# Retention and cross attention in a decoder step: the low weight parts on VectorE, the sample's rows turned later, the last products by token halves

## The chip, the cores and the metric

One core of one Trainium2 chip runs the whole step in one program. Its engines are TensorE (PE, with its weight loads as PEld), VectorE (DVE), ScalarE (ACT), GpSimd (POOL) and SyncE (SP, which only issues transfers here). Each engine works its own instructions in order and waits for others by semaphores. The metric is the device time of one execution in microseconds, lower is better.

## The reference

One step of a decoder of two layers, on 512 prompt tokens and 8 x 8 sample tokens, 576 token columns in all, with 1024 channels. Layer 0 mixes tokens by retention, layer 1 by causal pooling; each then attends to 256 memory tokens (cross attention, four heads of 256) and runs a gated feed-forward part with a short convolution. Cut to what bears on the change:

```python
def retention_mixer(h, pos, s0, w_in, gn_g, w_out):
    proj = h @ w_in                       # q, k, v, g of 4 heads
    q, k = rope(...), rope(...) * RET_DK ** -0.5
    o, s = retention_chunks(q, k, v, s0, chunk)      # chunks of 128 tokens
    o = ((o - mu) * lax.rsqrt(var + GN_EPS)).reshape(B, L, hv) * gn_g
    return (jax.nn.silu(g) * o) @ w_out, s

def cross_attn(h, k, v, wq, wo):
    q = (h @ wq).reshape(B, L, X_HEADS, X_HEAD_DIM)
    p = jax.nn.softmax(jnp.einsum('blhd,bmhd->bhlm', q, k) * X_HEAD_DIM ** -0.5, axis=-1)
    return jnp.einsum('bhlm,bmhd->blhd', p, v).reshape(B, L, D_MODEL) @ wo
```

All inputs and outputs are float32.

## The kernel before

Channels lie on the 128 partitions and tokens along the free axis, the 64 sample tokens first. A float32 product is made of three passes of a faster TensorE format: every operand is split into a high part (a cast, on ScalarE) and a low part (source minus high part), and `mm3` adds high x high, high x low and low x high. `split` writes both parts. `load_w` does it for each weight tile of 128x1024: a transfer to `wraw`, the cast to `wh` (L229), and the subtraction to `wl` (L230). The subtraction is on VectorE, except where `W.lo` is 1: there it is on GpSimd. `W.lo` is 1 while the tasks of a cross stage are run (L1184 to L1187), of which there are two, one per layer.

The 576 columns of a product are two pieces of PSUM, one of 320 (sample and the first 256 prompt tokens) and one of 256, called the token halves. `mm_kt` makes one step: one output tile of 128 channels, one 128-deep slice of the input, both halves, three passes: two `wh` matmuls and one `wl` matmul per half.

The order in which PE works is set by code. A main list of tasks (projections and the products that follow) hands over after every step, and side generators (`B` side of a head: the sample's recurrent state; out side: the prompt's chunks; in the cross stages one side per pair of heads) are called between them. A side says with `yield t` after how much estimated PE work, in microseconds, it wants to be called again; `Weave` keeps the clock of these estimates. A scheduler then places each engine's instructions; tiles of a pool with `bufs=n` can hold a program's instruction back until one of n slots is free.

In the retention the sides of head h end in the same way. `normed` (from L635) takes the statistics of a 128x512 result in PSUM on VectorE and writes the normed tile `on` on ScalarE (L642), with two slots. `gate_out` turns `on` by four transposes on PE (L219), multiplies it by the gate on VectorE into `yt`, and stores it (heads 0 to 2) or splits it into `qhl` and `khl` (head 3). The sample does this in `b_side`, each of four prompt chunks in `out_side`.

`out_tasks` is the product with `w_out`: four groups of two output tiles, and four parts of the input per group, one per head. The first group's fourth part uses head 3's fresh `qhl` and `khl`; its eight steps go output tile by output tile, each with both halves.

A cross stage computes the query tiles (`ev_q`: `qt` on VectorE, its split into `qo`, a copy of the sample's columns into `Z` on GpSimd), runs the attention of prompt and sample as sides (`ph`, `pl` are the parts of the turned probabilities or keys, `pT` the turned probabilities, `mx`, `sm` belong to the softmax), and multiplies by `w_xo`, which adds to the residual `x` (L1162, or L417 for whole tiles) and feeds the norm of the next stage (`sqacc` and `xhl`).

Of the kernel before, what the change touches and what calls it, by code (L numbers as in the profile page):

```python
# [156 lines left out]
def body(ctx, tc, a, cdec):  # L157
# [4 lines left out]
    def f(t):  # L162
        return t.bitcast(F32)
# [17 lines left out]
    def acc():  # L181
        return P.acc.tile([128, 1024], F32, tag="acc", name=nm("acc"))

    def tp():
        return P.tp.tile([128, 512], F32, tag="tp", name=nm("tp"))

    def new(p, shape, tag, dt=F32, whole=True, **kw):


        n = 1  # L190
        for s in shape[1:]:
            n *= s
        o = LINE // 2 if tag in ODD else 0
        if n % LINE == 0 and o == 0 or not whole:
            return p.tile(shape, dt, tag=tag, name=nm(tag), **kw)
        t = p.tile([shape[0], -(-(n + o) // LINE) * LINE], dt, tag=tag, name=nm(tag), **kw)[:, o:o + n]
        if len(shape) == 2:
            return t
        ax = "abcd"[:len(shape) - 1]
        return t.rearrange(f"p ({' '.join(ax)}) -> p {' '.join(ax)}", **dict(zip(ax[1:], shape[2:])))  # L200

    def token_rows(p, shape, tag):

        return new(p, shape + [ROW], tag, F32R)[:, :, :, ROW - NT:]
# [7 lines left out]
    def mm(out, lhsT, rhs, start, stop):  # L212
        i = nc.tensor.matmul(out, lhsT, rhs, start=start, stop=stop)  # L213
        if not wv.inside:
            wv.last = i.ins
        wv.now += max(cols(rhs) / 2340.0, 0.107)
# [5 lines left out]
    def mm3(out, lh, ll, rh, rl, start, stop):  # L222
        mm(out, lh, rh, start, False)
        mm(out, lh, rl, False, False)
        mm(out, ll, rh, False, stop)

    def split(hi, lo, src, scale=None, lo_pool=False):
        if scale is None:
            act.copy(hi, src)  # L229
            (pool if lo_pool else dve).tensor_tensor(out=lo, in0=src, in1=f(hi), op=ALU.subtract)  # L230
        else:
            act.activation(hi, src, AF.Copy, scale=scale)
            dve.scalar_tensor_tensor(out=lo, in0=src, scalar=scale, in1=f(hi), op0=ALU.mult, op1=ALU.subtract)  # L233
# [16 lines left out]

    class W:
        pool = first = None
        lo = 0

    def load_w(src, shape):

        raw = new(W.pool, shape, "wraw", bufs=W.raw_bufs)
        dma.dma_start(out=raw, in_=src)
        wh = new(W.pool, shape, "wh", F32R, bufs=W.hl_bufs)
        wl = new(W.pool, shape, "wl", F32R, bufs=W.hl_bufs)  # L260
        split(wh, wl, raw, lo_pool=W.lo)
        return wh, wl

    def w_cols(w, r0, nk, c0):
# [17 lines left out]
    def two_cols(w, *cs):  # L282
        return lambda: [w_cols(w, 0, KT, c) for c in cs]
# [130 lines left out]
    def add_x(norm=None):  # L414
        def evac(i, ps):
            x = xt["x"]
            dve.tensor_tensor(out=x[:, i], in0=x[:, i], in1=flat(ps), op=ALU.add)  # L417
            if norm is not None:
                norm.feed(i)
        return evac  # L420
# [216 lines left out]
    def normed(o):  # L637

        mv, rs, nb = gn_stats(o, 128)
        on = new(ap, [128, 512], "on", bufs=2)  # L640
        dve.tensor_scalar(out=nb, in0=mv[:, 0:1], scalar1=rs, scalar2=-1.0, op0=ALU.mult, op1=ALU.mult)
        act.activation(on, o, AF.Identity, scale=rs, bias=nb)  # L642
        return on
# [80 lines left out]
    def b_side(h):  # L724

        s = hd[h]
        vst = s["vst"]
        S = {}
        order = [(4 * g + j, k2) for g in range(2) for k2 in range(2) for j in range(4)]

        def state(t, u):
            b, k2 = order[u]
            return t[0, b, h, 128 * k2:128 * k2 + 128]

        def load(u):
            if u < 2 * B:
                S[u] = new(ap, [128, DV], "S", bufs=10)
                dma.dma_start(out=S[u], in_=state(a["state_ret"], u))

        for u in range(8):  # L740
            load(u)
        yield 4.5
        pso = tp()
        mm(pso, As, s["vs32"], True, False)
        yield 0.3
        for u in range(2 * B):
            b, k2 = order[u]
            if u % 4 == 0:
                for j in range(4):
                    c = 128 * (b // 4) + 32 * j  # L750
                    mm(pso[32 * j:32 * j + 32], Z[:, k2, c:c + 32], S[u + j], False, u == 2 * B - 4)
            psu = tp()
            mm(psu, kst[:, b, 128 * k2:128 * k2 + 128], vst[:, b // 4], True, True)
            Su = S.pop(u)
            dve.scalar_tensor_tensor(out=Su, in0=Su, scalar=cdec[h], in1=psu, op0=ALU.mult, op1=ALU.add)  # L755
            dma.dma_start(out=state(a["o_ret_s"], u), in_=Su)
            load(u + 8)
            yield 1.7
        on = normed(pso)
        yield 6.0  # L760
        gate_out(h, on, 0)

    def out_side(h):

        s = hd[h]
        A, vhl = s["A"], s["vhl"]
        ons = {}
        for qc in range(5):
            if qc < 4:
                ps = tp()  # L770
                for kc in range(qc + 1):
                    o = AOFF[kc] + 128 * (qc - kc)
                    mm3(ps, A[:, 0, o:o + 128], A[:, 1, o:o + 128], vhl[:, 0, kc], vhl[:, 1, kc], kc == 0, kc == qc)
                ons[qc] = normed(ps)
                yield 6.0
            if qc > 0:
                gate_out(h, ons.pop(qc - 1), NS + 128 * (qc - 1))
                yield 0.5
# [111 lines left out]
    def out_tasks():  # L890
        tasks = []
        evac = add_x(first_norm)
        for grp in range(4):
            hold = {}
            for part, k0 in enumerate((8, 0, 4, 12)):
                def run(wt, part=part, k0=k0, grp=grp, hold=hold):
                    if part == 0:
                        if grp == 0:
                            wv.join(hd[3]["y2"])
                        hold.update({0: acc(), 1: acc()})  # L900
                    if grp == 0 and part == 1:
                        ya = token_rows(gp, [128, 2, KT], "xhl")
                        for ft in range(8):
                            y_load(ft, ya[:, 0, ft], ya[:, 1, ft])
                    if grp == 0 and part == 3:
                        wv.join(hd[3]["out"], hd[3]["bl"])
                        for i in range(4):
                            yk[12 + i] = y3[i // 2][:, 0, i % 2], y3[i // 2][:, 1, i % 2]
                        sA.close()
                        xt["pool"] = xp = open_pool(sX, "xp")  # L910
                        xt["x"] = new(xp, [128, KT, NT], "x")
                        for kt in range(KT):
                            dma.dma_start(out=xt["x"][:, kt], in_=x_dram[:, kt])
                        W.pool = open_pool(sX, "wB")
                        W.raw_bufs, W.hl_bufs = 3, 3
                    wh, wl = wt
                    if grp == 3 and part == 3:
                        first_norm.gcol = G_XA
                        for kt in range(4):
                            first_norm.split(kt)  # L920
                    for m, kt in [(m, kt) for kt in range(4) for m in range(2)] if part < 3 else \
                            [(m, kt) for m in range(2) for kt in range(4)]:
                        cc = slice(128 * m, 128 * m + 128)
                        mm_kt(hold[m], (wh[:, :, cc], wl[:, :, cc]), kt, *yk[k0 + kt], part + kt == 0,
                              part == 3 and kt == 3)
                        yield
                        if part == 3 and kt == 3:
                            evac(2 * grp + m, hold[m])
                            if grp == 3 and m == 0:
                                first_norm.split(4)  # L930
                                first_norm.split(5)

                tasks.append(Task(lambda k0=k0, grp=grp: w_rows(w_out, 128 * k0, 4, 256 * grp, 256), run))
        return tasks

# [12 lines left out]
    def cross(l, norm, nnext):  # L948
        with ExitStack() as sp, ExitStack() as s:
# [231 lines left out]
            t0 = wo_tasks(0, (lambda: (wv.join(sides[0][0]), sides[1].append(wv.spawn(prompts_side(1)))),  # L1181
                              lambda: wv.join(*sides[0])))
            t1 = wo_tasks(1, (lambda: wv.join(sides[1][1]), lambda: wv.join(*sides[1])), nnext)
            W.lo = 1  # L1184
            wv.run(run_tasks(tasks + t0 + t1, two_cols(a["w_up"][l], 0, DFF)))
            wv.drain()
            W.lo = 0  # L1187


    def ffn(l, norm, nnext=None, side=None, then=None):  # L1190
# [370 lines left out]
```

## Time and profile before

| | us |
|---|---|
| median of 3 runs | 1900.1 |
| lowest, highest | 1899.54, 1905.7 |
| the profiled execution | 1899.72 |
| its span | 1897.9 |
| PE busy | 1859.6 |
| DVE busy | 1055.9 |
| ACT busy | 734.7 |
| POOL busy | 272.4 |

The span runs from the first to the last instruction of the profile. By place: retention heads from about 80 to 525 us, the product with `w_out` to 615, the first cross stage to 786, feed-forward 0 to 1150, memory and pooling to 1285, the second cross stage to 1464, feed-forward 1 to the end. An engine that is busy for nearly all of the span sets the time; for the others only the moments count at which that engine waits for them.

### The profile page before, as it was taken

Reading aid. Unit: us, or ns where it says so; the run is one execution under the profiler, and the core shown is the slowest. Engines: PE = TensorE matmul, PEld = TensorE weight load, DVE = VectorE, ACT = ScalarE, POOL = GpSimd, SP = SyncE. Lnnn points to the kernel's source line nnn. Section 1 sums busy time; section 2 is a strip of 40 time slices with the busy share of each in tenths; the row PEclk is TensorE's granted clock in tenths of the full one; section 3 lists DMA queues with packets and bytes.
Section 4 is the critical chain, followed back from the end, with each engine's and each line's share of the span. In section 5 each row is a group of like instructions: output and inputs, shape, how many; then the busy total and the mean of one; then the engine's idle time right before and its main releaser. Section 6 shows DMA issues by size and latency. Waiting matters only on the chain.

```text
span 1897.9 us, 32670 instructions
## 1 busy us (share of the span) xinstructions
PE 1859.6 (98%) x13493; PEld 1742.7 (92%) x13493; DVE 1055.9 (56%) x1607; ACT 734.7 (39%) x1080; POOL 272.4 (14%) x416
## 2 busy tenths in 40 slices
PE   7999999999999999999999999999999999999998
PEld 6888888888899888899999999988898999999998
DVE  5635445464634554676366367674555673564567
ACT  5442332424423433443234134554443442342345
POOL 0211102021000312211011010003212210110010
PEclk9999999999999999999999999999999999999999
DMA  8645363555733555232322322546543223232224
GB/s 288 206 135 177 97 217 114 173 163 159 242 111 105 170 176 167 79 101 79 89 87 82 90 78 76 182 139 212 188 157 115 84 79 89 80 87 86 82 73 142
DMA packets 309691, 249.52 MB, mean 131 GB/s; under 512 B 12136, under 2 KB 267992, under 8 KB 309543
## 3 DMA queue, kind: packets, MB, share of 16 engines
q1 hardware_dynamic: 309543, 247.44, 42.3%
q8 instruction: 106, 1.74, 0.4%
q14 instruction: 42, 0.34, 0.1%
HBM read 210.51 MB, written 36.88 MB: 130 GB/s over the span
## 4 chain that ended last, share of the span: by engine, by line
PE 88%; DMA 3%; DVE 3%; issue 2%; ACT 2%; POOL 1%; SPq 0%; ACTq 0%; POOLq 0%; DVEq 0%
PE acc L213 74%; PE tp L213 11%; PE tp L219 3%; DMA kvr<-in_cache_mem_v 1%; DMA wraw<-in_w_xk 1%; DVE qo L230 1%; ACT wh L229 1%; DVE wl L230 1%; DMA wraw<-in_w_xq 0%; DMA cs<-in_c_rope 0%; ACT qo L229 0%; DVE xhl L233 0%; DMA y<-in_p_conv 0%; POOL r L602 0%; POOL wl L230 0%
## 5 line engine op out<-in xcount | busy, mean ns | idle before, releaser
L213 PE MATMUL acc<-xhl,wh 128*128 128x320 f32 (+1 forms) x4608 | 919.6, 295 | 2.2 <-ACT m4k L473 1.0
L213 PEld LDWEIGHTS acc<-xhl,wh 128*128 128x128 f32 x4608 | 737.8, 188 | 13.4 <-issue 6.7
L213 PE MATMUL acc<-xhl,wl 128*128 128x320 f32 (+1 forms) x2304 | 674.8, 293 | 0.0
L229 ACT CAST wh<-wraw 128x1024 fp32r<-128x1024 f32 (+1 forms) x274 | 281.3, 1030 | 644.6 <-PE acc L213 508.9
L213 PEld LDWEIGHTS acc<-xhl,wl 128*128 128x128 f32 x2304 | 434.0, 188 | 0.0
L230 DVE TENSOR_TENSOR wl<-wraw,wh 128x1024 fp32r<-128x1024 f32 (+1 forms) x242 | 293.3, 1215 | 131.9 <-ACT wh L229 126.1
L213 PE MATMUL acc<-yhl,wh 128*128 128x320 f32 (+1 forms) x1408 | 278.7, 295 | 0.1
L213 PEld LDWEIGHTS acc<-yhl,wh 128*128 128x128 f32 x1408 | 223.7, 188 | 0.5 <-ACT yhl L229 0.4
L213 PE MATMUL acc<-yhl,wl 128*128 128x320 f32 (+1 forms) x704 | 205.8, 293 | 0.0
L1234 DVE SCALAR_TENSOR_TENSOR c<-e,cw,c 128x592 f32<-128x592 f32 x176 | 145.9, 832 | 3.8 <-ACT c L1232 0.3
L213 PEld LDWEIGHTS acc<-yhl,wl 128*128 128x128 f32 x704 | 132.6, 188 | 0.0
L417 DVE TENSOR_TENSOR x<-x,acc 128x576 f32<-128x576 f32 x64 | 48.2, 753 | 148.2 <-PE acc L213 148.0
L230 POOL TENSOR_TENSOR wl<-wraw,wh 128x1024 fp32r<-128x1024 f32 x32 | 78.5, 2452 | 287.0 <-ACT wh L229 247.7
L213 PE MATMUL acc<-qo,wh 128*128 128x320 f32 (+1 forms) x512 | 108.0, 305 | 6.1 <-DVE x L1162 5.5
L213 PE MATMUL acc<-wh,xhl 128*128 128x512 f32 (+1 forms) x320 | 96.4, 374 | 0.0
L213 PEld LDWEIGHTS acc<-qo,wh 128*128 128x128 f32 x512 | 82.2, 191 | 12.7 <-DVE x L1162 6.4
L213 PE MATMUL acc<-wh,mT 128*128 128x512 f32 x256 | 86.1, 405 | 3.1 <-ACT wh L229 3.1
L1232 ACT ACTIVATE c<-e,cw 128x592 f32<-128x592 f32 x88 | 77.6, 884 | 21.0 <-DVE e L1227 20.6
L1225 DVE TENSOR_TENSOR e<-acc,rstd_bc 128x64 f32<-128x64 f32 x88 | 19.5, 222 | 114.4 <-PE acc L213 114.2
L1228 POOL COPY cb<-e 128x16 f32<-128x16 f32 x88 | 18.8, 214 | 422.4 <-DVE e L1225 422.4
L213 PE MATMUL acc<-qo,wl 128*128 128x256 f32 (+1 forms) x256 | 75.8, 299 | 0.0
L755 DVE SCALAR_TENSOR_TENSOR S<-S,tp 128x512 f32<-128x512 f32 x64 | 43.6, 682 | 52.6 <-PE tp L213 46.7
(281 smaller groups left out, 2328.9 us busy)
## 6 DMA issues: line engine op xcount, KB each, us to landing
wraw<-in_w_up SPq DMA_DIRECT2D x88, 512.0 KB, 3.7
wraw<-in_w_ret_in SPq DMA_DIRECT2D x48, 512.0 KB, 4.4
S<-in_state_ret SPq DMA_DIRECT2D x64, 256.0 KB, 4.1
o_ret_s<-S SPq DMA_DIRECT2D x64, 256.0 KB, 3.5
kvr<-in_cache_mem_k SPq DMA_DIRECT2D x64, 256.0 KB, 4.1
kvr<-in_cache_mem_v SPq DMA_DIRECT2D x64, 256.0 KB, 3.5
wraw<-in_w_down SPq DMA_DIRECT2D x32, 512.0 KB, 3.8
wraw<-in_w_down SPq DMA_DIRECT2D x24, 384.0 KB, 3.3
```

Source lines behind the costliest of these rows:

```text
L213: i = nc.tensor.matmul(out, lhsT, rhs, start=start, stop=stop)
L219: nc.tensor.transpose(out, in_, idn)
L229: act.copy(hi, src)
L230: (pool if lo_pool else dve).tensor_tensor(out=lo, in0=src, in1=f(hi), op=ALU.subtract)
L417: dve.tensor_tensor(out=x[:, i], in0=x[:, i], in1=flat(ps), op=ALU.add)
L755: dve.scalar_tensor_tensor(out=Su, in0=Su, scalar=cdec[h], in1=psu, op0=ALU.mult, op1=ALU.add)
L1225: dve.tensor_tensor(out=ev[:, 0:8, 2:10], in0=ps[:, A0:A0 + NS].rearrange("p (b t) -> p b t", t=T), in1=rstd_bc[:, 0:NS].rearrange("p (b t ...
L1228: pool.tensor_copy(cb[:, 0:16, j].rearrange("p (b t) -> p b t", t=2), ev[:, 0:8, 8:10])
L1232: act.activation(c, e[:, 2:2 + n], AF.Identity, scale=cw[:, 2, j:j + 1], bias=cw[:, 3, j:j + 1])
L1234: dve.scalar_tensor_tensor(out=c, in0=e[:, i:i + n], scalar=cw[:, i, j:j + 1], in1=c, op0=ALU.mult, op1=ALU.add)
```

## The change

Three edits. First, `W.lo` goes: the low parts of the weights loaded in the cross stages are written by VectorE like all others, 32 tiles of 128x1024. Second, the numbers in the sides' `yield` change: the sample's rows are turned after 8.5 instead of 6.0 us of estimated PE work (5.0 in head 3), and the prompt's chunks of head 3 after 4.5 instead of 6.0. Third, the fourth part of the first group of `out_tasks` runs all its steps for the first token half and then all for the second.

```diff
--- before.py
+++ after.py
@@ -250,7 +250,6 @@
 
     class W:
         pool = first = None
-        lo = 0
 
     def load_w(src, shape):
 
@@ -258,7 +257,7 @@
         dma.dma_start(out=raw, in_=src)
         wh = new(W.pool, shape, "wh", F32R, bufs=W.hl_bufs)
         wl = new(W.pool, shape, "wl", F32R, bufs=W.hl_bufs)
-        split(wh, wl, raw, lo_pool=W.lo)
+        split(wh, wl, raw)
         return wh, wl
 
     def w_cols(w, r0, nk, c0):
@@ -757,7 +756,7 @@
             load(u + 8)
             yield 1.7
         on = normed(pso)
-        yield 6.0
+        yield 8.5 if h < 3 else 5.0
         gate_out(h, on, 0)
 
     def out_side(h):
@@ -772,7 +771,7 @@
                     o = AOFF[kc] + 128 * (qc - kc)
                     mm3(ps, A[:, 0, o:o + 128], A[:, 1, o:o + 128], vhl[:, 0, kc], vhl[:, 1, kc], kc == 0, kc == qc)
                 ons[qc] = normed(ps)
-                yield 6.0
+                yield 6.0 if h < 3 else 4.5
             if qc > 0:
                 gate_out(h, ons.pop(qc - 1), NS + 128 * (qc - 1))
                 yield 0.5
@@ -918,13 +917,19 @@
                         first_norm.gcol = G_XA
                         for kt in range(4):
                             first_norm.split(kt)
-                    for m, kt in [(m, kt) for kt in range(4) for m in range(2)] if part < 3 else \
-                            [(m, kt) for m in range(2) for kt in range(4)]:
+                    both = (0, 1)
+                    steps = [(m, kt, both) for kt in range(4) for m in range(2)]
+                    if part == 3:
+                        steps = [(m, kt, both) for m in range(2) for kt in range(4)]
+                        if grp == 0:
+
+                            steps = [(m, kt, (hv,)) for hv in both for m in range(2) for kt in range(4)]
+                    for m, kt, halves in steps:
                         cc = slice(128 * m, 128 * m + 128)
                         mm_kt(hold[m], (wh[:, :, cc], wl[:, :, cc]), kt, *yk[k0 + kt], part + kt == 0,
-                              part == 3 and kt == 3)
+                              part == 3 and kt == 3, halves)
                         yield
-                        if part == 3 and kt == 3:
+                        if part == 3 and kt == 3 and halves[-1]:
                             evac(2 * grp + m, hold[m])
                             if grp == 3 and m == 0:
                                 first_norm.split(4)
@@ -1181,10 +1186,8 @@
             t0 = wo_tasks(0, (lambda: (wv.join(sides[0][0]), sides[1].append(wv.spawn(prompts_side(1)))),
                               lambda: wv.join(*sides[0])))
             t1 = wo_tasks(1, (lambda: wv.join(sides[1][1]), lambda: wv.join(*sides[1])), nnext)
-            W.lo = 1
             wv.run(run_tasks(tasks + t0 + t1, two_cols(a["w_up"][l], 0, DFF)))
             wv.drain()
-            W.lo = 0
 
 
     def ffn(l, norm, nnext=None, side=None, then=None):
```

On PE in head 0, `on_278` is the sample's normed tile and `on_266` that of a prompt chunk. Before, the sample's transposes stand right behind the twelve `kdA` matmuls, and the next product steps (`acc` from `xhl`) behind them:

```order
L213 MATMUL tp_281_1755<-vhl_172_1054,kdA_189_1175 128x512 x12
L219 MATMUL tp_285_1777<-ident_2_64,on_278_1720 128x128 x4
L213 MATMUL acc_275_1707<-xhl_25_131,wh_256_1596 128x320 x2
L213 MATMUL acc_275_1707<-xhl_25_131,wl_257_1597 128x320
L213 MATMUL acc_275_1707<-xhl_25_131,wh_256_1596 128x256 x2
L213 MATMUL acc_275_1707<-xhl_25_131,wl_257_1597 128x256
```

Now three steps of this product and one of the next stand between; the transposes of `on_266` follow at once:

```order
L213 MATMUL tp_281_1755<-vhl_172_1054,kdA_189_1175 128x512 x12
L213 MATMUL acc_275_1707<-xhl_25_131,wh_256_1596 128x320 x2
L213 MATMUL acc_275_1707<-xhl_25_131,wl_257_1597 128x320
...
L213 MATMUL acc_290_1805<-xhl_25_131,wh_273_1703 128x320 x2
...
L213 MATMUL acc_290_1805<-xhl_25_131,wl_274_1704 128x256
L219 MATMUL tp_291_1812<-ident_2_64,on_278_1720 128x128 x4
L219 MATMUL tp_293_1821<-ident_2_64,on_266_1669 128x128 x4
```

The sample's transposes moved by four product steps; those of the prompt's chunk stand where they were.

On PE at the end of head 3, before, `on_741` is the sample's tile and `on_747` that of the last prompt chunk; `qhl_696` and `khl_697` are the parts of the gated rows, `wh_737` and `wl_738` the weight tile that they meet first:

```order
L213 MATMUL tp_744_4835<-vhl_622_4090,kdA_645_4226 128x512 x12
L219 MATMUL tp_748_4857<-ident_2_64,on_741_4797 128x128 x4
L213 MATMUL acc_702_4552<-xhl_718_4656,wh_716_4652 128x320 x2
...
L219 MATMUL tp_753_4893<-ident_2_64,on_734_4760 128x128 x4
L219 MATMUL tp_755_4904<-ident_2_64,on_747_4854 128x128 x4
L213 MATMUL acc_701_4551<-qhl_696_4543,wh_737_4781 128x320 x2
L213 MATMUL acc_701_4551<-qhl_696_4543,wl_738_4782 128x320
L213 MATMUL acc_702_4552<-qhl_696_4543,wh_737_4781 128x320 x2
...
L213 MATMUL acc_701_4551<-qhl_696_4543,wh_737_4781 128x256
```

Now `on_740` is the last prompt chunk and `on_747` the sample, with `wh_743` and `wl_744` as that tile; the last row is the first one with the 256 columns of the second half:

```order
L219 MATMUL tp_750_4850<-ident_2_64,on_740_4793 128x128 x4
L213 MATMUL acc_701_4551<-xhl_717_4648,wh_715_4644 128x320 x2
...
L219 MATMUL tp_752_4891<-ident_2_64,on_747_4830 128x128 x4
L213 MATMUL acc_702_4552<-xhl_717_4648,wh_715_4644 128x320 x2
...
L213 MATMUL acc_702_4552<-xhl_717_4648,wh_715_4644 128x256 x2
...
L213 MATMUL acc_701_4551<-qhl_696_4543,wh_743_4814 128x320
...
L213 MATMUL acc_701_4551<-qhl_696_4543,wl_744_4815 128x320
...
L213 MATMUL acc_701_4551<-khl_697_4544,wh_743_4814 128x320 x2
...
L213 MATMUL acc_701_4551<-qhl_696_4543,wh_743_4814 128x256 x2
```

The sample's rows are turned last, one step ahead of the first `qhl` product, and the second token half comes after all products of the first.

On VectorE in the first cross stage, where the first three query tiles (`qt`, `qo`) and the low part `pl` are written; before:

```order
L1123 TENSOR_TENSOR qt_827_5839<-acc_819_5712,rstd_bc_5_67 128x576
L230 TENSOR_TENSOR qo_812_5700<-qt_826_5828,qo_812_5700 128x576
L230 TENSOR_TENSOR qo_812_5700<-qt_827_5839,qo_812_5700 128x576
L1123 TENSOR_TENSOR qt_834_5903<-acc_831_5850,rstd_bc_5_67 128x576
L230 TENSOR_TENSOR qo_812_5700<-qt_834_5903,qo_812_5700 128x576
L230 TENSOR_TENSOR pl_841_5927<-tp_839_5921,ph_840_5926 128x512
```

Now three `wl` stand among them:

```order
L1128 TENSOR_TENSOR qt_827_5839<-acc_819_5712,rstd_bc_5_67 128x576
L230 TENSOR_TENSOR qo_812_5700<-qt_826_5828,qo_812_5700 128x576
L230 TENSOR_TENSOR wl_830_5847<-wraw_828_5844,wh_829_5846 128x1024
L230 TENSOR_TENSOR qo_812_5700<-qt_827_5839,qo_812_5700 128x576
L230 TENSOR_TENSOR wl_837_5911<-wraw_835_5908,wh_836_5910 128x1024
L1128 TENSOR_TENSOR qt_834_5903<-acc_831_5850,rstd_bc_5_67 128x576
L230 TENSOR_TENSOR wl_855_6030<-wraw_853_6027,wh_854_6029 128x1024
L230 TENSOR_TENSOR qo_812_5700<-qt_834_5903,qo_812_5700 128x576
L230 TENSOR_TENSOR pl_841_5927<-tp_839_5921,ph_840_5926 128x512
```

Each `wl` that POOL had taken now has a place in VectorE's order ahead of a `qo` or a `qt`; nothing else on these rows moved.

## Rows read from the trace of the kernel before

**Rows 1.** The page, busy us (share of span) xinstructions of each engine

```profile
PE 1859.6 (98%) x13493; PEld 1742.7 (92%) x13493; DVE 1055.9 (56%) x1607; ACT 734.7 (39%) x1080; POOL 272.4 (14%) x416
```

**Rows 2.** What PE waited for: engine, line, us in total, times, longest

```profile
PE acc L213 <- DVE x L1162: 5.5, 2, 2.8
PE tp L219 <- ACT on L642: 3.9, 3, 1.3
...
PE acc L213 <- ACT qhl L229: 2.4, 1, 2.4
PE tp L213 <- DVE pl L230: 2.2, 2, 1.1
PE tp L213 <- DVE pT L230: 2.1, 2, 1.0
...
PE tp L219 <- DVE pl L230: 1.0, 2, 0.5
```

**Rows 3.** Windows: length, busy us (instructions) per engine, PEclk, DMA share, GB/s

```profile
526.00:529.50 3.50, 3.14 (x13) 3.14 (x14) 0.76 (x2) 0.61 (x2) 0.00 (x0) 0.51 0.25 87
771.00:776.90 5.90, 3.16 (x24) 2.96 (x22) 5.86 (x5) 1.61 (x3) 2.96 (x2) 1.00 0.36 102
1454.40:1457.90 3.50, 3.50 (x17) 3.50 (x16) 2.17 (x4) 1.86 (x4) 0.00 (x0) 0.51 0.33 98
```

**Rows 4.** Timeline, PE, head 0: start, us, line, op, xcount [idle before <-releaser]

```profile
192.02 0.66 PE L219 MATMUL tp<-ident,on 128*128 128x128 f32 x4 [1.28 <-ACT on L642]
...
195.70 0.60 PE L219 MATMUL tp<-ident,on 128*128 128x128 f32 x4
```

**Rows 5.** Timeline, ACT, head 0

```profile
191.19 0.78 ACT L642 ACTIVATE on<-tp,gn 128x512 f32<-128x512 f32 x1 [2.58 <-DVE gn L641]
194.40 0.78 ACT L642 ACTIVATE on<-tp,gn 128x512 f32<-128x512 f32 x1 [2.43 <-DVE gn L641]
```

**Rows 6.** Timeline, PE, end of head 3

```profile
519.16 0.60 PE L219 MATMUL tp<-ident,on 128*128 128x128 f32 x4
...
526.36 1.04 PE L213 MATMUL acc<-qhl,wh 128*128 128x256 f32 x3 [2.35 <-ACT qhl L229]
```

**Rows 7.** Timeline, ACT, end of head 3

```profile
520.54 0.30 ACT L229 CAST qhl<-yt 128x128 fp32r<-128x128 f32 x1 [1.74 <-DVE yt L627]
```

**Rows 8.** The page, groups: xcount, busy us, mean ns, idle before, releaser

```profile
L230 DVE TENSOR_TENSOR wl<-wraw,wh 128x1024 fp32r<-128x1024 f32 (+1 forms) x242 | 293.3, 1215 | 131.9 <-ACT wh L229 126.1
...
L417 DVE TENSOR_TENSOR x<-x,acc 128x576 f32<-128x576 f32 x64 | 48.2, 753 | 148.2 <-PE acc L213 148.0
L230 POOL TENSOR_TENSOR wl<-wraw,wh 128x1024 fp32r<-128x1024 f32 x32 | 78.5, 2452 | 287.0 <-ACT wh L229 247.7
```

**Rows 9.** Windows, the first cross stage, columns as in rows 3

```profile
620.00:780.00 160.00, 153.85 (x1288) 137.17 (x1287) 81.40 (x137) 63.15 (x129) 37.86 (x22) 1.00 0.49 153
```

**Rows 10.** Timeline, POOL, first cross stage

```profile
632.05 0.24 POOL L1125 COPY Z<-qt 128x64 f32<-128x64 f32 x1 [1.19 <-DVE qt L1123]
632.24 2.44 POOL L230 TENSOR_TENSOR wl<-wraw,wh 128x1024 fp32r<-128x1024 f32 x1
```

**Rows 11.** Timeline, DVE, first cross stage

```profile
632.75 2.53 DVE L230 TENSOR_TENSOR qo<-qt,qo 128x576 fp32r<-128x576 f32 x1 [0.77 <-ACT qo L229]
635.21 0.68 DVE L230 TENSOR_TENSOR pl<-tp,ph 128x512 fp32r<-128x512 f32 x1
```

**Rows 12.** Tile qo by form: min/median/max ns, first and last start

```profile
L230 DVE TENSOR_TENSOR qo<-qt,qo x8: 784/2484/2585, 625.3 to 697.4; 128x576 fp32r<-128x576 f32 x8
```

**Rows 13.** Timeline, DVE, end of the first cross stage

```profile
769.77 2.39 DVE L233 SCALAR_TENSOR_TENSOR xhl<-x,gv,xhl 128x576 fp32r<-128x576 f32 x1
...
772.75 3.04 DVE L233 SCALAR_TENSOR_TENSOR xhl<-x,gv,xhl 128x576 fp32r<-128x576 f32 x1
...
776.39 0.47 DVE L1162 TENSOR_TENSOR x<-x,acc 128x320 f32<-128x320 f32 x1
777.71 0.82 DVE L233 SCALAR_TENSOR_TENSOR xhl<-x,gv,xhl 128x576 fp32r<-128x576 f32 x1 [0.85 <-ACT xhl L232]
```

## The prediction

> **What bounds the kernel now.** Read the page's busy line first: PE works 98% of the span and nothing else comes near [rows 1]. No change in the diff takes a matmul away, so only PE's idle time and its slow stretches can be won. The span is 1897.9 us, the profiled execution 1899.72, so 1.8 us lie around the span; the median of the runs is 1900.1, or 0.4 above the profiled one.
>
> Next the table of what PE waited for, which names the engine and line that came last [rows 2]. Six of its lines stand at places that the diff touches: 5.5 us on VectorE's residual add `x` (two waits), 3.9 on ScalarE's `on` (three), 2.4 on `qhl` (one), 2.2, 2.1 and 1.0 on VectorE's `pl` and `pT` (two each). Together 17.1 us, 0.9% of the span: that is the size of what is at stake, apart from the clock. The clock comes third: over 526.0 to 529.5 and over 1454.4 to 1457.9 the granted clock is 0.51, which is the 1.2 GHz level, while it is 1.00 in the stretch that holds the wait at 773.9 [rows 3]. Each of the two slow stretches follows one of the long waits (the end of head 3, and the end of the second cross stage). At half speed 3.5 us do the work of 1.75, so each costs about 1.7 us, my estimate from those rows.
>
> **B: the sample's rows turned later (three of four heads).** Before, the four transposes of the sample's `on` come straight behind twelve `kdA` matmuls. ScalarE's `on` starts at 191.19 and takes 0.78, so it ends at 191.97; PE has been idle for 1.28 when the transposes start at 192.02 [rows 4, 5]. The new order puts four product steps between them. Steps are two 128x320 and two 128x256 pieces of three matmuls in all, about 0.8 us each by the distance of the transposes at 195.70 from those at 192.02 (four steps and the transposes themselves). That is more than twice the 1.28, so this wait goes: 3.9 us for three heads. What is late next: `on` has two buffers, so the following `on` can only be written when the sample's has been read. In before it is written 194.40 to 195.18, while PE wants it at 195.70 [rows 4, 5]. With the slot freed some 3 us later, but everything on PE 1.3 earlier, I see it ready about when PE asks; I take 0.1 off per head. B gives 3.6, with ends 0 (the wait only passes to the next `on`) and 3.9. The cover is product work that PE has to do anyhow; without it the 1.28 come back.
>
> **C: end of head 3.** Here the sample's transposes come last, one step ahead of the first products of the out projection, and these products run through the first token half (sample and 256 tokens) before the second. Before, PE stood 2.35 us for `qhl` at 526.36 and then ran the slow stretch [rows 6, 3]. The last quarter of `qhl` is now wanted eight half steps (three 128x320 each) later, so the 2.35 go, and with them probably the drop: 2.35 + 1.7 = 4.05 gross. New waits: from the start of the sample's transposes to its `qhl` there went 519.16 to 520.54 plus 0.30, or 1.7 us [rows 6, 7], and PE now has 0.35 of transposes and one step of 0.8, so about 0.4 is left open, more for the low half behind it. The trace has no row for the crowding ahead of it (the two `on` chains of head 3 come closer together than in other heads). Its ends: nothing, and the 2.35 that stood there before, with the drop again. The nearest row is the single `on` wait of the same kind, 1.3. I take 0.4 + 1.3 = 1.7. Net C 2.35, ends 0 and 4.05.
>
> **A: low parts from POOL to VectorE in the cross stages.** 32 tiles leave POOL, where each takes 2452 ns, and go to VectorE, where the same form takes 1215 ns: 16 tiles and 19.4 us more per stage, 39 us in all, for an engine that was busy for 81.4 of 160 us in the first one [rows 8, 9]. There is room on average; what counts is the order at the sites where PE waits.
>
> Take the first. POOL starts `wl` at 632.24; VectorE starts `qo` at 632.75 and needs 2.53 us for it, though the shortest of these eight took 784 ns; then `pl` at 635.21, for which PE waits 1.1 [rows 10 to 12, 2]. Of the eight, the median is 2484 ns. The long ones lie beside a POOL `wl`: this one ends at 635.28, 0.60 behind POOL's end at 634.68. With `wl` on VectorE the order there is `wl`, `qo`, `pl`. `wh` is ready by 632.24, while VectorE idles for 0.77 until `qo`'s high part comes, so `wl` runs to 633.46 and `qo` starts 0.71 later but is 1.75 shorter. Gain 1.0 of the 1.1. The `pT` site reads the same (1.0), the third (`pl`, 0.5) goes wholly. Both stages: 2.0 + 2.0 + 1.0 = 5.0.
>
> At the end of each stage `x` waits behind two `xhl` of 2.39 and 3.04 us, which take 0.82 where POOL is quiet [rows 13]. That is 3.8 too long. On VectorE there now come ahead of this `x` one `wl` (1.22) and one residual add that has been moved up (753 ns) [rows 8]: 3.8 - 1.22 - 0.75 = 1.8 per stage, of a wait of 2.75. The remaining 1 us is of the size of the waits of 1.0 to 1.3 elsewhere, and the clock is 1.00 over the whole first stage, which holds three of these [rows 9], so the slow stretch at 1454.4 goes too: 1.7. A is 5.0 + 3.6 + 1.7 = 10.3. Ends: 12.5 (all of the waits and the drop), and below nothing: if the long operations are not POOL's doing, each of the eight sites gets 1.22 of `wl` in front, 9.8 us lost.
>
> What the row shows is a `qo` that ends 0.60 behind POOL's `wl`, nearly its whole 0.78. The Trainium skill, page "SBUF — State Buffer", section "Who interferes with whom", puts it as a rule: a VectorE instruction with two SBUF inputs contends with a GpSimd instruction that reads SBUF, and the one that comes second is held until the other has finished. It speaks against this change as well, since the moved `wl` has two SBUF inputs and POOL still copies `Z` (0.24 at 632.05 [rows 10]). By that rule up to four such copies per stage could hold a `wl` that a site waits for, 8 x 0.24 = 1.9 us, and the time would be about 1885; by the rows alone it is the sum below. The trace agrees with the rule at this one place.
>
> **Sum.** B 3.6 + C 2.35 + A 10.3 = 16.25. After a wait the first instruction also takes longer (transposes 0.66 against 0.60 [rows 4]): eleven times 0.06 make 0.7. So 16.9 off the profiled 1899.72 is 1882.8, and 0.4 to the median: 1883.
>
> **The rivals.**
>
> First, VectorE becomes the releaser and the cross stages give nothing. For it: VectorE works in order, a `wl` that waits for its `wh` holds up everything behind it, and the sites are just those where VectorE came last. Against it: the shortest `qo` (784 ns) and the `xhl` of 0.82, both at times when POOL was doing no `wl` or had begun after them. Then only 16.9 - 10.3 = 6.6 is won: 1893.5.
>
> Second, the retention part gives nothing: the wait at `on` passes to the next `on` through its two buffers, and the end of head 3 keeps its wait and its slow stretch. For it: at the end of head 3 transposes, gate, `qhl` and products follow one another through PE, VectorE and ScalarE with little product work between them; against it: `on` was ready at 191.97 and is now wanted over 3 us later. 16.9 - 3.6 - 2.35 = 10.9: 1889. The clock belongs here: a wait of 2.35 was followed by a drop and one of 2.76 was not, so a shorter wait may still be followed by one, at 1.7 each. The Trainium skill, page "TensorE: Matmul & The Clock Gate", section "Part 1: The HAM clock gate", says that the activity window runs freely; by that rule the same wait may or may not bring a drop, and two drops would put the time at 1886. These rows agree that the length of a wait alone doesn't decide it.
>
> Third, slower than before: the moved `wl` stand ahead of evacuations all through the cross stages, not at eight sites only, because their weights arrive when PE hands over a slot and VectorE's queue then stands. At 1.22 each it takes ten of the 32 to eat the 6.6 that the retention brings and to be 0.3% slower (12.3 us); with sixteen of 32 in the way the time is 1899.7 + 19.5 - 6.6 = 1913. For it: 39 us more on one in-order queue. Against it: half of that engine's time is idle there, and a stretched instruction costs more than the `wl` that replaces it.
>
> Fourth, the edits cancel out and nothing is seen: 1900. For it: some of the waits passed on, as above, at both ends.
>
> **How the numbers follow.** The forecast (1878 to 1889) 0.66; second rival 0.10; first 0.13; fourth 0.05; third 0.06. What this kernel's measurement can tell from no change is 0.3%, 5.7 us, so faster means under 1894.4. The forecast and the second rival lie there, and 0.09 of the first's 0.13, which makes 0.85; the rest of it and the fourth are the same, 0.09; slower is 0.06. The range goes down to 1877: all gross terms, 3.9 + 4.05 + 12.5 + 0.7 = 21.2 or 1879, and 2 for waits not priced. It goes up to 1895, so that the first rival is in; 0.15 above it is left out.
>
> **What would show it.** In PE's table of waits the lines on `on` and on `pT` are gone, `x` is at about 2 us in two, `qhl` is under 1. VectorE's `qo` from `qt` are near 0.8 us all eight. No granted clock near 0.5 before the last 5 us. B is wrong if a wait of 1 us on `on` stands at another set of transposes; A is wrong if the waits on `pl` and `x` stay and `wl` on VectorE stands in front of them; the sum is wrong if new lines of 1 us or more appear in the table.

## The result: 1879.7 us, and the profile after

The changed kernel takes 1879.74 us (median of 4 runs, 1878.13 to 1883.23), the kernel before beside it 1900.68: a ratio of 0.9885 with a 95% interval of 0.9871 to 0.9898, so 21 us or 1.1% less. Forecast were 1883 and 1877 to 1895. The profiled execution took 1879.21, its span is 1877.4.

The page's busy line of the changed kernel, and its group of the low parts on VectorE (xcount, busy us, mean ns, idle before):

```profile
PE 1853.2 (99%) x13493; PEld 1740.2 (93%) x13493; DVE 1058.4 (56%) x1639; ACT 735.0 (39%) x1080; POOL 199.2 (11%) x384
...
L230 DVE TENSOR_TENSOR wl<-wraw,wh 128x1024 fp32r<-128x1024 f32 (+1 forms) x274 | 332.5, 1217 | 136.2 <-ACT wh L229 130.2
```

Beside [rows 1] and [rows 8]: the 32 `wl` have come over at 1217 ns, and yet VectorE is busy for 1058.4 us in place of 1055.9, because what was stretched is short again (the 16 `qo` from `qt` take 12.2 us in all in place of 35.1, the `xhl` 32.9 in place of 43.4). POOL fell from 272.4 to 199.2, PE's share rose to 99%. What PE waited for now (us in total, times, longest):

```profile
PE acc L213 <- ACT wh L229: 3.6, 2, 2.5
PE acc L213 <- DVE x L416: 1.9, 2, 0.9
...
PE acc L213 <- DVE r L600: 0.7, 1, 0.7
PE tp L213 <- ACT on L641: 0.7, 1, 0.7
```

None of the six lines of [rows 2] is left. New are two waits of 0.94 on a residual add, one of 0.7 on VectorE's `r` (the rope's result), one of 0.7 on `on`, and smaller ones; the line on `wh` stood in the table before too and is not the change's.

The first `pl` site (timeline of VectorE, then of PE; start, us, line, operation, xcount):

```profile
627.16 1.22 DVE L230 TENSOR_TENSOR wl<-wraw,wh 128x1024 fp32r<-128x1024 f32 x1 [0.19 <-ACT wh L229]
628.30 0.75 DVE L230 TENSOR_TENSOR qo<-qt,qo 128x576 fp32r<-128x576 f32 x1
628.97 0.68 DVE L230 TENSOR_TENSOR pl<-tp,ph 128x512 fp32r<-128x512 f32 x1
```

```profile
629.55 0.28 PE L213 MATMUL tp<-ph,qo 128*128 128x256 f32 x1
629.71 0.39 PE L213 MATMUL tp<-pl,qo 128*128 128x256 f32 x1
```

`wl`, `qo`, `pl` run in the order that the prediction read, and `pl` ends at 629.65, just as PE comes to it: the wait of 1.1 is gone [rows 11, 2]. All eight `qo` from `qt` are short (min/median/max ns), where the median was 2484 [rows 12]:

```profile
L230 DVE TENSOR_TENSOR qo<-qt,qo x8: 744/755/794, 620.3 to 690.6; 128x576 fp32r<-128x576 f32 x8
```

At the end of the first cross stage (VectorE, then PE):

```profile
763.02 0.81 DVE L233 SCALAR_TENSOR_TENSOR xhl<-x,gv,xhl 128x576 fp32r<-128x576 f32 x1
...
764.42 0.48 DVE L1167 TENSOR_TENSOR x<-x,acc 128x320 f32<-128x320 f32 x1
...
773.64 0.76 DVE L416 TENSOR_TENSOR x<-x,acc 128x576 f32<-128x576 f32 x1 [0.95 <-PE acc L213]
```

```profile
773.33 0.28 PE L213 MATMUL acc<-qo,wl 128*128 128x256 f32 x1
774.54 0.54 PE L213 MATMUL acc<-xhl,wh 128*128 128x320 f32 x2 [0.94 <-DVE x L416]
```

The `x` that PE had waited for, 776.39 in [rows 13], is now written at 764.42 and PE doesn't wait for it at all; it waits 0.94 further on, for the very last residual add at 773.64, whose accumulator the next stage takes first. And the clock behind the waits that are left (windows as in [rows 3], the third column from the right is the granted clock) stays at its upper level, 2.4 GHz:

```profile
508.60:512.10 3.50, 3.25 (x14) 2.68 (x15) 3.03 (x7) 1.47 (x4) 0.00 (x0) 1.00 0.22 82
774.40:777.90 3.50, 3.36 (x25) 3.39 (x26) 3.50 (x5) 1.87 (x3) 0.00 (x0) 1.00 0.74 197
1444.60:1448.10 3.50, 3.37 (x26) 3.40 (x27) 3.50 (x5) 1.87 (x3) 0.00 (x0) 1.00 0.49 133
```

To see where the time went, PE's products into `acc` are counted in both traces, and the stretches between the same counts are compared, in us of the profiled executions:

| stretch (count of products) | before | after | A alone | B alone | C alone | halves alone | two steps |
|---|---|---|---|---|---|---|---|
| 250 to 1250, end of head 0 | 219.22 | 218.54 | 220.55 | 219.06 | 219.28 | 218.86 | 216.69 |
| 1250 to 1750, end of head 1 | 112.16 | 110.69 | 112.18 | 110.69 | 112.17 | 112.23 | 110.64 |
| 1750 to 2500, heads 2 and 3 | 153.71 | 149.86 | 153.88 | 152.87 | 150.89 | 149.93 | 148.50 |
| 2500 to 4000, first cross stage | 277.73 | 269.99 | 270.01 | 279.77 | 277.49 | 279.51 | 270.17 |
| 4000 to 7000, feed-forward, memory | 400.55 | 400.56 | 400.57 | 400.54 | 400.56 | 400.56 | 400.54 |
| 7000 to 8500, second cross stage | 292.38 | 284.72 | 285.87 | 291.88 | 293.56 | 291.30 | 285.21 |

Ahead of product 250 the start of the program varies from one execution to the next (74.0 to 79.3 us in these traces); from 8500 to 10750 all take 293.51 us, and the last 450 products within 0.2 us the same, but for 0.6 more in A alone. So the change gave 6.0 us in the retention and 7.7 in each cross stage. Each column is one execution, and what it happened to wait for beside the change is in it: A's first row holds a wait of 2.0 on the first `r`, and B's trace is its slowest run of twelve (1903.95).

### The profile page after: what moved, and what is told of

The parts are those of the page before. It is cut to its first block, busy times and chain, and to the rows that moved or that the text cites. A ratio compares the mean times of both kernels' runs of the same rounds, so it can differ in the third digit from the quotient of the medians.

```text
span 1877.4 us, 32680 instructions
## 1 busy us (share of the span) xinstructions
PE 1853.2 (99%) x13493; PEld 1740.2 (93%) x13493; DVE 1058.4 (56%) x1639; ACT 735.0 (39%) x1080; POOL 199.2 (11%) x384
## 4 chain that ended last, share of the span: by engine, by line
PE 92%; issue 3%; DMA 2%; DVE 1%; ACT 1%; SPq 0%; POOL 0%; POOLq 0%; ACTq 0%; DVEq 0%
PE acc L213 77%; PE tp L213 11%; PE tp L219 3%; DMA wraw<-in_w_xk 1%; DMA wraw<-in_w_xq 0%; DMA cs<-in_c_rope 0%; DVE wl L230 0%; DMA y_dram<-yt 0%; DMA kvr<-in_cache_mem_v 0%; ACT wh L229 0%; DMA yr<-y_dram 0%; ACT m4k L472 0%; ACT z L229 0%; SPq L474 0%; POOL gn L342 0%
## 5 line engine op out<-in xcount | busy, mean ns | idle before, releaser
L230 DVE TENSOR_TENSOR wl<-wraw,wh 128x1024 fp32r<-128x1024 f32 (+1 forms) x274 | 332.5, 1217 | 136.2 <-ACT wh L229 130.2
L1235 ACT ACTIVATE c<-e,cw 128x592 f32<-128x592 f32 x88 | 77.6, 884 | 20.8 <-DVE e L1230 20.3
L213 PEld LDWEIGHTS acc<-wh,xhl 128*128 128x128 f32 x320 | 58.0, 188 | 11.4 <-issue 1.1
L1276 ACT ACTIVATE c<-c 128x592 f32<-128x592 f32 x44 | 30.8, 700 | 86.3 <-DVE c L1237 86.3
```

Source lines behind the costliest of these rows:

```text
L1235: act.activation(c, e[:, 2:2 + n], AF.Identity, scale=cw[:, 2, j:j + 1], bias=cw[:, 3, j:j + 1])
L1276: act.activation(c, c, AF.Silu)
```

## The experiments

**A alone.** The kernel before with one edit:

```diff
-            W.lo = 1
+            W.lo = 0
```

> Only the first edit: the low parts of the cross stages' weights go to VectorE, the retention stays as it was. Theory of the prediction, mended by the account by place: the waits on pl, pT and x go because VectorE is no longer held beside POOL, and the second cross stage's slow stretch goes with its long wait; the two stages then give about 7.7 us each, so about 1885 (15 us faster), with every qo from qt near 0.76 us. By the prediction's own sum (10.3) it would be 1890. Rival: part of the 15 us between the two profiles is chance in the arrival of kvr, and only the waits named go: 1888 to 1890, with waits on kvr as before (about 1.5 us over 692 to 756).

Measured: 1887.46, before 1901.87; ratio 0.9914 (0.9897 to 0.9932), 14 us by the medians. Its waits of PE:

```profile
PE tp L219 <- ACT on L642: 3.9, 3, 1.3
...
PE acc L213 <- ACT qhl L229: 2.4, 1, 2.4
...
PE acc L213 <- DVE x L417: 1.9, 2, 0.9
```

The retention's waits are there as before, the cross stages' are gone, and the two of 0.94 on the last residual add have come: these belong to A. By place it gives 7.7 and 6.5. The theory held on the waits that it named. On `kvr` (rows of the sample's memory as they are loaded) the rival named chance. Why PE (with its weight loads) sat idle at instructions on `kvr` from 640 to 765 us, first here, then in a kernel whose `wl` are on POOL (C alone):

```profile
  DMA kvr<-in_cache_mem_v: 0.7, 2
```

```profile
  DMA kvr<-in_cache_mem_v: 1.9, 4
```

The idle time alone doesn't tell: it is 1.6 to 1.9 in the four kernels with `wl` whole on POOL, and on VectorE 0.7 here, 1.1 in the changed kernel, 0.2 when that ran again, but 1.7 in the last kernel below. The stretch does: from product 3250 to 3500 the four with `wl` on POOL take 69.93 to 70.63 us, these four 68.41 to 69.08. So there is a gain of 1 to 2 us there, in the first cross stage only. That the raw weights' buffers come free sooner, and so the loads behind them on SyncE's queue, is what I take for the cause; it was not tried by itself.

**B alone.**

```diff
         on = normed(pso)
-        yield 6.0
+        yield 8.5 if h < 3 else 6.0
```

> Only the sample's transposes of heads 0 to 2 later (8.5 in place of 6.0). Theory: the three waits of 1.3 on ScalarE's on go and none comes in their place, 3 x 1.45 = 4.3 us, about 1896.4. Rival: in head 0 the gain is given back at the next head's rope (0.8 us on VectorE's r at 203.9, seen in the changed kernel's profile), since VectorE gets the sample's gate later there: 3.5 us, 1897.2. The profile decides: a wait on r of 0.6 or more between 195 and 210, or none.

Measured: 1898.40 against 1901.87; ratio 0.9974 (0.9961 to 0.9988), 3.5 us. The rival was right on head 0. VectorE there (timeline):

```profile
201.38 0.68 DVE L623 TENSOR_TENSOR yt<-tp,sg 128x512 f32<-128x512 f32 x1
207.62 0.69 DVE L623 TENSOR_TENSOR yt<-tp,sg 128x512 f32<-128x512 f32 x1 [5.56 <-DMA y_dram<-yt]
...
208.89 0.75 DVE L601 TENSOR_TENSOR r<-acc,cs 128x576 f32<-128x576 f32 x1
```

The prompt's `yt` at 207.62 waits 5.56 us for a transfer, the store of an earlier `yt`, and holds up the rope's `r` behind it, for which PE waits 0.84. The changed kernel shows it in its own trace (VectorE, then PE, then what idled for the store in all, over the retention):

```profile
196.37 0.48 DVE L626 TENSOR_TENSOR yt<-tp,sg 128x128 f32<-128x128 f32 x2
196.77 0.68 DVE L622 TENSOR_TENSOR yt<-tp,sg 128x512 f32<-128x512 f32 x1
202.83 0.69 DVE L622 TENSOR_TENSOR yt<-tp,sg 128x512 f32<-128x512 f32 x1 [5.38 <-DMA y_dram<-yt]
203.44 0.75 DVE L599 TENSOR_TENSOR rt<-acc,cs 128x576 f32<-128x576 f32 x1
204.10 0.75 DVE L600 TENSOR_TENSOR r<-acc,cs 128x576 f32<-128x576 f32 x1
```

```profile
205.00 0.47 PE L213 MATMUL acc<-wh,xhl 128*128 128x512 f32 x1 [0.66 <-DVE r L600]
```

```profile
  DMA y_dram<-yt: 13.1, 3
```

`yt` has two buffers. Turned four steps later, the sample's rows (196.37) fall right beside a prompt chunk's (196.77), and a third comes before the first is stored. This happens in each of the three heads (13.1 us of idle time on VectorE), but only in head 0 does PE come to want what is queued behind. Heads 1 and 2 give 1.47 each, head 0 only 0.2 to 0.7. (B's row for heads 2 and 3 shows 0.84, since its slow stretch behind `qhl` began 0.8 us after that wait's end, and before the change 0.3 ahead of it, in idle time.)

**C alone, and the token halves alone.** C is the kernel before with the edits of the change that touch the end of head 3 (the sample of heads 0 to 2 stays at 6.0); the second kernel takes C's new yields back and keeps only the order of the steps:

```diff
-        yield 6.0 if h < 3 else 5.0
+        yield 6.0
...
-                yield 6.0 if h < 3 else 4.5
+                yield 6.0
```

> Only the end of head 3: its three earlier transposes and the first token half ahead of the second. Theory: the wait of 2.35 on qhl and the slow stretch behind it go (4.2 us with the restart), and about 1.2 come back as a wait on on ahead of kdA and a small one on qhl: 3 us, about 1897.7. Rival: the slow stretch is not tied to this wait and stays somewhere in 500 to 560: 1.3 us, about 1899.4.

> The token halves without the new yields in head 3: sample and prompt chunks are turned where they were before. Theory: the last rows ready before are those of the last prompt chunk, which belong to the second half, so the halves alone take the wait on qhl and the slow stretch away, and without the tighter yields the wait on on ahead of kdA (0.65) isn't there either: 4 us, about 1896.7, a little better than with the yields. Rival: the yields are what brings qhl in time, and the halves alone still wait 1 us or more for qhl: 1898.5 or later.

Measured: C 1899.00 (ratio 0.9976, 0.9964 to 0.9988), the halves alone 1898.01 (0.9973, 0.9961 to 0.9985), before 1901.87. The two intervals overlap; the place decides, in one profile each: heads 2 and 3 take 2.8 us less in C and 3.8 less with the halves alone. No wait on `qhl` of any size is left without the new yields, and 0.12 us with them. The rival, a slow stretch that stays, fell: the granted clock is 1.00 from 500 to 560 us, in C and with the halves alone (columns as in [rows 3]):

```profile
500.00:560.00 60.00, 59.50 (x427) 56.39 (x426) 33.28 (x59) 21.66 (x33) 2.58 (x4) 1.00 0.50 168
```

```profile
500.00:560.00 60.00, 60.00 (x433) 56.93 (x432) 33.25 (x59) 21.64 (x33) 3.27 (x4) 1.00 0.52 171
```

With the new yields there is a wait on `on` ahead of `kdA` (C alone):

```profile
PE tp L213 <- ACT on L642: 0.3, 1, 0.3
```

In the changed kernel it is 0.65 (0.94 when that ran again); there `on` stands on ScalarE behind a cast that waited for `yr`, stored rows that are read back (PE, then ScalarE):

```profile
508.85 3.05 PE L213 MATMUL tp<-vhl,kdA 128*128 128x512 f32 x12 [0.65 <-ACT on L641]
```

```profile
507.45 0.67 ACT L229 CAST xhl<-yr 128x576 fp32r<-128x576 f32 x1 [3.40 <-DMA yr<-y_dram]
508.03 0.77 ACT L641 ACTIVATE on<-tp,gn 128x512 f32<-128x512 f32 x1
```

So the order by token halves is what won. That the tighter yields took some of it back rests on the traces: 1 us here, and 1.4 to 1.6 between the changed kernel and the last one below; the two times don't resolve it. These two runs, which still have both waits of 2.76 on `x`, also say what the clock does behind them. C alone, then the halves alone, the 3.5 us behind the wait in the first and in the second cross stage:

```profile
774.90:778.40 3.50, 3.27 (x25) 3.27 (x26) 2.33 (x4) 1.65 (x3) 0.00 (x0) 1.00 0.43 130
1453.00:1456.50 3.50, 3.29 (x13) 3.29 (x14) 2.31 (x4) 1.66 (x3) 0.00 (x0) 0.53 0.47 138
```

```profile
772.80:776.30 3.50, 3.27 (x13) 3.27 (x14) 2.33 (x4) 1.64 (x3) 0.00 (x0) 0.50 0.49 141
1452.50:1456.00 3.50, 3.28 (x25) 3.28 (x26) 2.32 (x4) 1.66 (x3) 0.00 (x0) 1.00 0.45 134
```

The same wait at the same place is followed by the 1.2 GHz level in one stage and not in the other, and which one changes from run to run: in the four kernels of this study that have both waits (before, B, C, the halves) it was one of the two each time, 4 of 8. It lasts 3.4 us each time in the second stage (before, C) and 6.8 each time in the first (B, the halves), where it costs twice as much. Behind `qhl`'s 2.36 it was 3 of 3 (before, A, B). Behind single waits up to 1.5 it was none, but for the last 10 us of the program.

**Low parts on POOL in pieces.** The changed kernel, with the cross stages' `wl` back on POOL (`W.lo` is 1 there as it was before the change):

```diff
-        split(wh, wl, raw)
+        if W.lo:
+            act.copy(wh, raw)
+            fl = [t.rearrange("p a b -> p (a b)") for t in (wl, raw, f(wh))]
+            for j in range(8):
+                o, i0, i1 = [t[:, 128 * j:128 * j + 128] for t in fl]
+                pool.tensor_tensor(out=o, in0=i0, in1=i1, op=ALU.subtract)
+        else:
+            split(wh, wl, raw)
...
```

> The changed kernel with the cross stages' low parts back on POOL, each written by eight instructions of 128x128 in place of one of 128x1024. The same data are read and written on POOL, and VectorE does no more than before the change. Theory: a VectorE instruction with two SBUF inputs is held until the POOL instruction in front of it ends, so it now loses at most one short piece: qo from qt at 0.8 to 1.2 us, the waits on pl, pT and x nearly gone, about 1882 (within 3 us of the changed kernel). Rival: the two engines share bandwidth, so what counts is how long POOL works beside VectorE: qo stays at 2 us or more, the waits stay, and only the retention's edits are won: about 1895.

Measured: 1898.43 against 1901.92 (ratio 0.9976, 0.9963 to 0.9989). The time went as the rival said, or worse, but not for its reason. `qo` in the first cross stage (min/median/max ns):

```profile
L230 DVE TENSOR_TENSOR qo<-qt,qo x8: 759/1022/4117, 620.0 to 693.0; 128x576 fp32r<-128x576 f32 x8
```

Seven of the eight take 0.76 to 1.09 us, and all eight of the second stage 0.82 to 1.09; each ends 0.6 us behind the end of a piece. So VectorE does get in between two pieces, as the theory had it, and is not slowed in proportion to POOL's time. The eighth takes 4.12. VectorE, then POOL, at that place:

```profile
627.50 4.12 DVE L230 TENSOR_TENSOR qo<-qt,qo 128x576 fp32r<-128x576 f32 x1 [0.85 <-ACT qo L229]
631.54 0.68 DVE L230 TENSOR_TENSOR pl<-tp,ph 128x512 fp32r<-128x512 f32 x1
```

```profile
627.44 0.24 POOL L1138 COPY Z<-qt 128x64 f32<-128x64 f32 x1
627.63 3.37 POOL L266 TENSOR_TENSOR wl<-wraw,wh 128x128 fp32r<-128x128 f32 x8
```

It starts while POOL copies `Z`, and ends 0.62 behind the last of eight pieces that follow back to back. PE waited 2.76 for the `pl` behind it and got the slow clock. The pieces are also dear: 531 ns each on average, 4.2 us for a tile in place of 2.45, and PE waits for transfers, 2.36 and 1.77 of it in two waits for `y`, again with the slow clock behind each; why these transfers are late was not tried. So the time went to one long `qo`, to transfers and to the clock, in parts that the runs don't separate. The run tells that POOL's instruction in front is what holds VectorE, and that cutting it up in this way doesn't keep the gain.

**Every low part twice.**

```diff
         split(wh, wl, raw)
+        if W.lo:
+            dve.tensor_tensor(out=wl, in0=raw, in1=f(wh), op=ALU.subtract)
...
```

> The changed kernel with every low part of the cross stages written twice on VectorE, the second time with the same result: 39 us more on that engine. Theory: half of VectorE's time in these stages is free and the second writing is placed behind what PE waits for next, so waits appear only where a second wl stands ahead of qo, pl, pT or x: up to 1.2 us at up to eight sites, 1880 to 1888. Rival (the third one of the prediction): its order is the limit, and every second writing pushes an evacuation: 32 x 1.2 = 39, 1905 or more.

Measured: 1884.12 (ratio 0.9901, 0.9886 to 0.9917), beside the changed kernel's 1880.19: 39 us more on VectorE cost 3.9. The second writing stands behind `pl` at the first site:

```profile
627.63 0.74 DVE L230 TENSOR_TENSOR qo<-qt,qo 128x576 fp32r<-128x576 f32 x1
628.29 0.68 DVE L230 TENSOR_TENSOR pl<-tp,ph 128x512 fp32r<-128x512 f32 x1
628.90 1.21 DVE L263 TENSOR_TENSOR wl<-wraw,wh 128x1024 fp32r<-128x1024 f32 x1
```

The theory held: VectorE has room. What the second writing costs shows as single waits of PE, 1.28 us on the last residual add of the second stage (0.94 without it), and two new ones of 1.07 on a `wh` and 1.00 on a `qt` at the end of the first.

**The changed kernel again,** without an edit, in the same group of runs:

> The changed kernel itself, as it stands, beside the others of this group: about 1880, so that the others can be compared with it on one chip.

Measured: 1880.19 against 1901.92; ratio 0.9881 (0.9864 to 0.9899).

**Two steps in place of four, and the old yields in head 3.**

```diff
-        yield 8.5 if h < 3 else 5.0
+        yield 7.2 if h < 3 else 6.0
...
-                yield 6.0 if h < 3 else 4.5
+                yield 6.0
```

> The changed kernel with other numbers in the yields: the sample's rows of heads 0 to 2 are turned two product steps later than before in place of four (7.2 in place of 8.5), and in head 3 the sides keep the numbers of before, with the token halves left in. Theory: on is ready some 0.1 us before PE comes to it, the sample's store of yt goes out sooner, the third yt holds VectorE up for less, and head 0's wait on r (0.8) goes; in head 3 the wait on on ahead of kdA (0.65) goes. About 2 us less than the changed kernel, 1878. Rival: the wait on r has another cause than the store of yt and stays, or the transposes wait again for on by 0.3 us or more in each head: no gain, 1880.

Measured: 1877.09 (1876.04 to 1878.77), beside 1880.19 (1879.50 to 1881.71) for the changed kernel: 3.1 us less, and the two sets of runs don't overlap. By place it takes 2.8 us less in the retention than that kernel's trace, 3.3 less than the changed kernel's in the table. Two lines of its table of waits, and VectorE in head 0:

```profile
PE acc L213 <- DVE x L416: 1.9, 2, 0.9
PE acc L213 <- DVE wl L230: 1.9, 3, 0.8
```

```profile
195.66 1.28 DVE L622 TENSOR_TENSOR yt<-tp,sg 128x512 f32<-128x512 f32 x2
...
201.06 0.75 DVE L600 TENSOR_TENSOR r<-acc,cs 128x576 f32<-128x576 f32 x1
```

There is no line on `r`, `on` or `qhl` in that table any more. The two prompt `yt` run in one go and `r` comes at 201.06 without a wait for a store. This is the best kernel of the study; what it has left on the changed places is A's pair of 0.94.

## Why the prediction was right

It was right in sign and, in the main, in mechanism, and the time is 3.3 us below the 1883 that it named: the gain is 20.9 us where the sum has 16.9. The 4 us are A's, which measured more than the upper end that the prediction gave it. Alone, the three parts give 14.4 + 3.5 + 2.9 = 20.8 us against 20.9 together; the intervals of the three leave some 5 us for an interaction, and none is seen.

- **B, 3.6 forecast, 3.5 measured.** The waits on `on` went, as read. The size agrees partly by chance: I took 0.1 off per head for `on`'s two buffers, which cost nothing, and missed `yt`'s two buffers, which cost 0.8 in head 0 (the last kernel took that wait away by turning these rows two steps earlier than the change does). The prediction counted the transposes that are moved, but not the store that goes with them and the slot that it keeps; that was the step that failed.
- **C, 2.35 forecast, 2.9 measured** (2.8 by place). Gross 4.05 and new waits, 1.7 forecast and 0.8 found (0.65 on `on`, 0.12 on `qhl`, as gaps in the changed kernel); the halves alone, which have neither wait, give 3.8 gross. The prediction named the crowding of the `on` chains, but not the cast that `on` stands behind on ScalarE, and the halves alone show that the wait need not have been there.
- **A, 10.3 forecast, 14.4 measured alone,** 14.2 by place there and 15.4 in the changed kernel, above the upper end of 12.5. The mechanism was right, a term was mis-sized and one missing. `pl` and `pT` gave all 5.3 in place of 5.0, and a restart that was larger than the 0.06 I took: from start to start PE now takes 0.16 us in place of 1.38 at the first site, 1.22 less, where the table says 1.10, and the three sites of a stage give 3.0 to 3.3 in place of 2.5. Missing was `kvr`: between products 3250 and 3500 the first stage became 1.6 us shorter (70.59 to 68.95), where [rows 2] has no wait, since PE's weight loads were the ones that waited. For `x` the 1.8 per stage came out right by two errors: the wait went wholly (2.75), and 0.94 came back at the stage's last evacuation, which the prediction didn't see.
- **The clock.** The drop in the second stage went with its wait. But its 1.7 is no fixed term of that place: each of the four kernels with both waits of 2.76 paid for one of them in its trace, now the first, now the second, and in the first 3.4. Over all runs it is more. Each run has its mean granted clock, and what that lacks of 1, times the span, is an estimate of the time that the 1.2 GHz level cost (the slow last 5 to 8 us of every trace included). Beside A alone the kernel before lacks 8.1 us on average (29 runs, granted clock 0.993 to 0.998), A alone 4.1 (six runs), so about 4 of A's gain is the clock, where the sum has 1.7. The time of the kernel before goes with it: its five runs at a granted clock of 0.994 took 1907.0 us on average, its ten at 0.997 took 1900.2.
- **`Z` copies in front of a moved `wl`,** priced at up to 1.9 us beside the sum: none of it is seen, VectorE's `wl` take 1.21 to 1.26 from 599 to 776 us of the changed kernel. The copies are held instead, the longest for 1.3 us in place of 0.24, and PE waits for none of them. The Trainium skill's rule ("SBUF — State Buffer", "Who interferes with whom"), by which the later of the two is held until the other ends, agrees with this and with 15 of the 16 `qo` in pieces; the one of 4.12 us waited for more than one instruction.
- **The third rival** (VectorE's order as the bound) fell with the doubled low parts, the first with A alone, the second with C and B alone, each faster with an interval that excludes 1.

## What to carry to other kernels

Where two engines slow each other, price the move by the instructions that are held, at the places where the bound engine waits, and not by the busy time that changes hands: 39 us more of work moved onto VectorE came out as 14 us less in all. Whoever moves a step later must look at what it stores, too: the buffer that its transfer keeps can stop the whole engine behind it. And of an edit in several parts each is worth its own run; here one part, by the traces, was better left undone.

## What was not expected of the hardware

A VectorE instruction that waits for POOL is not sure of the next turn: with POOL's work in pieces of about 0.45 us it got in behind one of them in 15 of 16 cases, and in one it waited through a copy and eight pieces, 4.12 us in all. And whether PE's clock falls to 1.2 GHz behind a wait of 2.4 to 2.8 us is not a matter of the wait alone: 3 of 3 behind one, 4 of 8 behind the other. Of the shorter waits one of 1.77 (for `y`, in pieces) was followed by it, and one of 1.66 with one of 0.77 close behind (on weights, when the changed kernel ran again); one of 2.04 (on `r`, A alone) was not. Single waits up to 1.5 never were, but for the last 10 us of the program.
